# Two more transposes of a decoder trunk moved from TensorE to DMA, and one product of the norm weights moved ahead

## The chip, the core and the metric

The kernel runs on one core of a Trainium2 chip. A core has five engines that each work through their own list of instructions in order and wait for each other through semaphores: TensorE (PE, matrix products and transposes into PSUM), VectorE (DVE), ScalarE (ACT), GpSimd (POOL) and SyncE (SP, which here only issues DMA transfers). The metric is the time of one execution in microseconds (us); less is better.

## The reference

One layer: a norm, one wide projection, two branches (multi-scale pooling, sliding-window attention with a sink), one output projection, a second norm and a residual. 1024 tokens, width 1024, 8 heads of 64, two key/value heads. Cut to what is computed:

```python
h = rmsnorm(x, norm_pre)
pool_u, pool_gate, q, k, v, attn_gate = split(h @ w_in)
pool_out = pool_mixer(pool_u, pool_w, pool_scale) * silu(pool_gate)
# 128-query blocks, keys of this block and of the one before, ALiBi bias, a sink logit per head
probs = softmax(concat([scores + bias, sink]))[..., :-1]
attn_out = (probs @ v) * silu(attn_gate)
y = concat([pool_out, attn_out]) @ w_out
x = x + rmsnorm(y, norm_post)
```

## The kernel before, in words

Everything between x and y is kept transposed, channels on the 128 partitions and tokens along the free axis. To keep float32 accuracy at float16 speed, each operand of a large product is split into a high and a low float16 part (a scaled copy on ACT, then the difference on DVE), and each product is three passes (high*high, high*low, low*high).

**Tokens.** x comes in eight tiles of 128 tokens. `norm_scan` (ACT, with a small DVE and a small POOL step behind it) and `norm_scale` (DVE, line 241) normalize a tile to `h`. `flip` (line 250) transposes it on PE in float32, eight 128x128 blocks into two PSUM banks. `land_hi` (ACT, line 254) and `land_lo` (DVE, line 261) take it from there into `hT`, the float16 pair that all projections read.

**Weights.** A slice of `w_in` (128 columns) is loaded, its absolute sum taken on ACT (`bound_w`, line 91), spread over the partitions by a PE transpose (`spread`, line 82), and turned on DVE into a power of two (`scale_w`, lines 87 to 77, 213). Then ACT writes the high part (`high_w`, line 219) and DVE the low part (`low_w`, line 223).

**Units.** The projection is cut into 34 units `proj(ch, half)`: 24 matmuls of 128x512 at line 290 into one of the two PSUM banks of `ps_acc`. Unit s+2 therefore can't start before unit s has been taken out of its bank (`land_slot`; for a q slice by ACT and then DVE, lines 94 and 95). Units 0 to 4 are k and the four q slices for tokens 0 to 511, units 5 to 9 the same for tokens 512 to 1023, then pool gates, pool inputs (u) and attention gates. `v_tile` (line 272) makes v for one token tile.

**Attention.** From unit 5 on, two units carry one block n of 128 queries: `score_mm` (PE), `score_land` (DVE, lines 369 to 380), `exps` (ACT, line 387), `turn` and `turn_low` (ACT line 397, DVE line 402), which make a float16 pair of the probabilities. One DMA transpose on SP (line 406) turns it into `full`. POOL cuts out the two masked parts (`mask`, lines 425 and 429). PE multiplies by v (`pv_mm`, line 453) into the one bank of `ps_pv`. The reciprocals of the softmax sums are spread by POOL to 128x512 (line 411), turned on PE in float32 through the same `ps_pv` bank (`divide`, line 440), and copied by ACT with v's scale into `cat` (line 441). `pv_land` (DVE, line 463) multiplies both.

**Order.** The order on each engine is the order in which the code is written (`manual_schedule`); no scheduler changes it. `middle()` runs between the two halves of a unit's matmuls: weight scales, `divide` and the pooling products (`mixed`, line 506) stand there. Of the pooling branch, DVE makes window sums (lines 489 to 501), and the product of a slice needs the last of them.

## Time and profile before

| | before |
|---|---|
| time, median of 3 runs | 345.78 us (345.5 to 347.47) |
| the profiled execution, its own time | 346.77 us |
| its span, first to last instruction | 345.1 us |
| PE busy | 323.6 us, 94% of the span |
| DVE, ACT, POOL busy | 199.1, 168.9, 66.2 us |
| mean granted TensorE clock | 0.989 of full speed |

A share of 94% says that PE seldom stands still, not that it alone sets the end: an engine that is 50% busy can be the late one in a stretch where it and a third engine wait for each other in turn. So the profile is read by stretches, with the question which wait ends last. All times in the rows below are counted from the start of the span.

### The profile page before, as it was taken

What the parts mean: (1) busy time and instruction counts of PE and PEld (TensorE: products, weight loads), DVE (VectorE), ACT (ScalarE), POOL (GpSimd) and SP (SyncE); (2) the same over time, 40 slices, a digit from 0 to 9 for tenths busy, and PEclk for the clock granted to TensorE, in tenths of its full rate; (3) what the DMA queues carried; (4) which work ended last, traced back from release to release, by engine and by line L of the source; (5) the groups of instructions that cost most, each with busy time, mean ns of one, the idle gap of its engine ahead of it and who ended that gap; (6) DMA issues with size and microseconds to landing.
All of it is one profiled execution on the core that took longest, in us unless ns stands there. A gap on an engine that the chain in (4) does not pass through costs nothing.

```text
span 345.1 us, 5054 instructions
## 1 busy us (share of the span) xinstructions
PE 323.6 (94%) x1913; PEld 166.4 (48%) x1913; DVE 199.1 (58%) x423; ACT 168.9 (49%) x368; POOL 66.2 (19%) x73
## 2 busy tenths in 40 slices
PE   4689999999999999999979998799999999999993
PEld 2588556545444445445434443344444444444442
DVE  4976771537697445796979567793563633410222
ACT  4966831275656685878484443354463433211011
POOL 1100303000132344050423000000000333212330
PEclk9969999999999999999999999999999999999999
DMA  7986240001437367395240892010000241233111
GB/s 280 255 230 159 86 123 0 2 19 44 122 122 208 120 164 179 66 181 126 62 122 0 291 245 76 0 63 0 0 2 0 68 150 59 90 123 122 61 63 61
DMA packets 52090, 35.73 MB, mean 104 GB/s; under 512 B 35041, under 2 KB 45793, under 8 KB 52066
## 3 DMA queue, kind: packets, MB, share of 16 engines
q1 hardware_dynamic: 52064, 35.40, 37.1%
q8 instruction: 15, 0.25, 0.3%
q14 instruction: 9, 0.07, 0.1%
q10 hardware_dynamic: 2, 0.00, 0.0%
HBM read 27.01 MB, written 4.19 MB: 90 GB/s over the span
## 4 chain that ended last, share of the span: by engine, by line
PE 46%; DVE 19%; issue 16%; ACT 9%; POOL 6%; DMA 2%; POOLq 0%; DVEq 0%; SPq 0%; ACTq 0%
PE acc L290 30%; POOL o L639 5%; ACT st L387 4%; PE pv L272 3%; PE y L272 3%; DVE whl L223 3%; DVE st L375 2%; PE tp L250 2%; DVE win L489 2%; PE acc L272 2%; PE sc L358 2%; DVE sc L374 2%; DVE o L636 2%; PE pvo L453 1%; DVE negm L380 1%
## 5 line engine op out<-in xcount | busy, mean ns | idle before, releaser
L290 PE MATMUL acc<-hT,whl 128*128 128x512 f16 x792 | 176.7, 379 | 1.1 <-ACT gt L529 1.1
L290 PEld LDWEIGHTS <-whl 128*128 128x128 f16 x792 | 76.6, 98 | 93.9 <-issue 8.3
L272 PE MATMUL y<-wo,chl 128*128 128x512 f16 (+2 forms) x408 | 83.6, 366 | 0.0
L272 PEld LDWEIGHTS <-chl 128*128 128x128 f16 x408 | 39.0, 98 | 43.5
L219 ACT ACTIVATE whl<-wraw,ws 128x1024 f16<-128x1024 f32 x18 | 20.4, 1148 | 34.6 <-DVE wu L213 22.4
L609 ACT ACTIVATE junk<-y 128x512 bf16<-128x512 f32 (+2 forms) x17 | 9.7, 572 | 54.9 <-PE y L272 54.9
L387 ACT ACTIVATE st<-st,negm 128x129 f32<-128x129 f32 x64 | 24.8, 390 | 12.6 <-DVE negm L380 9.6
L611 DVE SCALAR_TENSOR_TENSOR eps_of<-yss,eps_of 128x1 f32<-128x1 f32 x17 | 3.2, 185 | 45.9 <-ACT junk L609 45.9
L631 POOL TENSOR_TENSOR yf<-eps_of,mhalf 128x1 f32<-128x1 f32 x7 | 3.9, 551 | 119.2 <-DVE eps_of L611 119.2
L223 DVE SCALAR_TENSOR_TENSOR whl<-wraw,ws,whl 128x1024 f16<-128x1024 f32 x18 | 23.7, 1327 | 0.0
L402 DVE SCALAR_TENSOR_TENSOR ph<-st,ph 128x1024 f16<-128x1024 f32 x8 | 9.8, 1226 | 21.6 <-ACT ph L397 21.6
L91 ACT ACTIVATE whl<-wraw 128x1024 bf16<-128x1024 f32 x18 | 18.8, 1049 | 1.5 <-DMA wraw<-in_w_in_dram 1.5
L639 POOL TENSOR_TENSOR o<-o,xr 128x512 f32<-128x512 f32 x14 | 17.5, 1269 | 9.1 <-DVE o L636 9.1
L425 POOL TENSOR_SCALAR_AFFINE_SELECT own<-full 128x2048 f16<-128x2048 f16 x7 | 14.5, 2071 | 22.9 <-DMA full<-ph 22.9
L411 POOL COPY r<-sums 128x512 f32<-128x512 f32 x8 | 4.9, 612 | 67.7 <-DVE sums L409 45.8
L250 PE MATMUL tp<-ident,h 128*128 128x128 f32 x64 | 10.9, 331 | 6.6 <-DVE h L241 3.4
L95 DVE SCALAR_TENSOR_TENSOR chl<-cat,cs,chl 128x1024 f16<-128x1024 f32 x8 | 10.3, 1284 | 10.2 <-ACT chl L94 10.2
L94 ACT ACTIVATE chl<-cat,cs 128x1024 f16<-128x1024 f32 x8 | 9.2, 1148 | 13.7 <-DVE cs L77 13.7
L375 DVE SCALAR_TENSOR_TENSOR st<-sc,qu,bias 128x256 f32<-128x256 f32 x32 | 15.2, 484 | 1.0
L429 POOL TENSOR_SCALAR_AFFINE_SELECT full<-full 128x2048 f16<-128x2048 f16 x7 | 14.4, 2055 | 0.5
L250 PEld LDWEIGHTS tp<-ident,h 128*128 128x128 f32 x64 | 9.1, 172 | 7.9 <-DVE h L241 3.8
L358 PE MATMUL sc<-kT,qT 64*128 64x256 f16 (+1 forms) x192 | 11.6, 263 | 0.6 <-DVE qT L95 0.4
(109 smaller groups left out, 371.9 us busy)
## 6 DMA issues: line engine op xcount, KB each, us to landing
wraw<-in_w_in_dram SPq DMA_DIRECT2D x10, 512.0 KB, 5.1
x<-in_x_dram SPq DMA_DIRECT2D x8, 512.0 KB, 5.4
wraw<-in_w_in_dram SPq DMA_DIRECT2D x16, 256.0 KB, 4.6
woraw<-in_w_out_dram SPq DMA_DIRECT2D x8, 512.0 KB, 5.5
woraw<-in_w_out_dram SPq DMA_DIRECT2D x16, 256.0 KB, 6.8
xr<-in_x_dram SPq DMA_DIRECT2D x8, 512.0 KB, 3.7
out_dram<-o SPq DMA_DIRECT2D x16, 256.0 KB, 2.0
post<-in_norm_post_dram SPq DMA_DIRECT2D x1, 512.0 KB, 4.2
```

The lines of the kernel that those rows point to most:

```text
L91: nc.scalar.activation(junk, src, AF.Abs, accum_out=m)
L219: nc.scalar.activation(whl[ch][:, 0], raws[ch], AF.Copy, scale=halves[ch])
L223: nc.vector.scalar_tensor_tensor(w[:, 1], raws.pop(ch), s, w[:, 0], op0=ALU.mult, op1=ALU.subtract)
L250: nc.tensor.transpose(flips[tt][b][:, block_of(i)], h[:, block_of(4 * b + i)], ident)
L272: nc.tensor.matmul(acc, a, b, start=i == 0, stop=i == len(pairs) - 1)
L290: nc.tensor.matmul(acc, w[:, a, k, :], hT[:, b, k, half_of(half)], start=k == 0 and i == 0, stop=k == KT - 1 and i == 2,)
L358: nc.tensor.matmul(banks[kv][:, ci, k0:, :], qT[rows, a, 2 * pr + ci, block_of(n)], kT[rows, b, (n - 1 + k0) * P : (n + 1) * P], start=i = ...
L375: nc.vector.scalar_tensor_tensor(st[:, hs, :P], sc[:, :, 0 if n else 1, :], qu[:, 2 * pr : 2 * pr + 1], (bias if n else bias0)[:, hs, :], ...
L387: nc.scalar.activation(st[:, h, :], st[:, h, :], AF.Exp, bias=negm[:, h : h + 1], accum_out=sums[:, h : h + 1],)
L425: nc.gpsimd.affine_select(o, f, pattern=[[0, 16], [1, P]], compare_op=ALU.is_ge, fill=0.0, base=0, channel_multiplier=-1,)
L429: nc.gpsimd.affine_select(f, f, pattern=[[0, 16], [-1, P]], compare_op=ALU.is_ge, fill=0.0, base=-1, channel_multiplier=1,)
L639: nc.gpsimd.tensor_tensor(o[:, hs], o[:, hs], xr[:, hs], op=ALU.add)
```

## The change

Three edits.

1. `gains()`: the product that spreads the norm weights' maximum stands between the products of the two halves of the weights, and on DVE the copy of the second half stands behind the three small scale operations.
2. Token tiles 4 to 7 are no longer turned on PE. `swing` makes the float16 pair first (ACT cast, DVE difference, both in SBUF) and turns it by one DMA transpose straight into `hT`. The steps around it are written in another order, and the three small loads of constants stand behind the last of these transposes on SP.
3. The reciprocals are scaled by 4096, split into a float16 pair on POOL, spread (two copies), turned by a DMA transpose, and added up by POOL into `cat`. PE's transposes and ACT's copy go away; v's scale is applied in `pv_land`.

```diff
-        for half in range(2):
-            nc.tensor.matmul(rows[half], ones, pre[:, half_of(half)], start=True, stop=True)
+        nc.tensor.matmul(rows[0], ones, pre[:, half_of(0)], start=True, stop=True)
         nc.tensor.matmul(most, ones, m, start=True, stop=True)
+        nc.tensor.matmul(rows[1], ones, pre[:, half_of(1)], start=True, stop=True)
         nc.vector.tensor_copy(grow[:, half_of(0)], rows[0])
-        nc.vector.tensor_copy(grow[:, half_of(1)], rows[1])
 ...
+        nc.vector.tensor_copy(grow[:, half_of(1)], rows[1])
 ...
+    def swing(tt):
+        h = h_tiles.pop(tt)
+        hh = work("hh").bitcast(F16).rearrange("p (a d) -> p a d", a=2)
+        nc.scalar.copy(hh[:, 0], h)
+        nc.vector.tensor_tensor(hh[:, 1], h, hh[:, 0], op=ALU.subtract)
+        nc.sync.dma_start_transpose(
+            hT[:, :, :, block_of(tt)].rearrange("p a k t -> p (a k) t"),
+            hh.rearrange("p a d -> p (a d)"),
+        )
 ...
         nc.vector.reciprocal(sums, sums)
-        r = t2.tile([P, 512], F32, tag="t2", name="r")
-        nc.gpsimd.tensor_copy(
-            r.rearrange("p (c kv d) -> p c kv d", c=4, kv=2),
-            sums.rearrange("p (kv c) -> p c kv", kv=2).unsqueeze(3).broadcast_to([P, 4, 2, HD]),
+        nc.gpsimd.tensor_scalar(r8, sums, 4096.0, 0.0, op0=ALU.mult, op1=ALU.add)
+        nc.gpsimd.tensor_copy(rp[:, 0], r8)
+        nc.gpsimd.tensor_tensor(rp[:, 1], r8, rp[:, 0], op=ALU.subtract)
+        r = t2.tile([P, 2, 512], F16, tag="t2", name="r")
+        for a in range(2):
+            nc.gpsimd.tensor_copy(
+                r[:, a].rearrange("p (c kv d) -> p c kv d", c=4, kv=2),
+                rp[:, a].rearrange("p (kv c) -> p c kv", kv=2).unsqueeze(3)
+                .broadcast_to([P, 4, 2, HD]),
+            )
+        rt = t2.tile([P, 2, 512], F16, tag="t2", name="rt")
+        nc.sync.dma_start_transpose(
+            rt.rearrange("p a (c t) -> p (a c) t", t=P), r.rearrange("p a j -> p (a j)")
         )
 ...
     def divide(n):
-        r = att_r.pop(n)
-        rb = ps_pv.tile([P, 512], F32, tag="pv", name="rb")
-        for c in range(4):
-            nc.tensor.transpose(rb[:, block_of(c)], r[:, block_of(c)], ident)
-        nc.scalar.activation(
-            cat[:, 4:8, block_of(n)], rb.rearrange("p (c t) -> p c t", t=P), AF.Copy, scale=vo
-        )
+        rt = att_r.pop(n).rearrange("p a (c t) -> p a c t", t=P)
+        nc.gpsimd.tensor_tensor(cat[:, 4:8, block_of(n)], rt[:, 0], rt[:, 1], op=ALU.add)
 ...
-        nc.vector.tensor_tensor(dst, pv.rearrange("p (c t) -> p c t", t=P), dst, op=ALU.mult)
+        nc.vector.scalar_tensor_tensor(
+            dst, pv.rearrange("p (c t) -> p c t", t=P), vo, dst, op0=ALU.mult, op1=ALU.mult
+        )
 ...
         low_w(QS[1])
-        load_constants()
         v_tile(0)
 ...
         bound_w(QS[2])
+        swing(4)
         norm_scale(5)
         unit(1)
         bound_w(QS[3])
         norm_scan(6)
         spread_w((QS[2], QS[3]))
-        flip(4)
-        flip(5)
-        norm_scan(7)
+        swing(5)
         norm_scale(6)
-        land_hi(4)
-        land_hi(5)
         scale_w((QS[2], QS[3]))
-        land_lo(4)
         high_w(QS[2])
         high_w(QS[3])
+        norm_scan(7)
+        low_w(QS[2])
         unit(2)
-        land_lo(5)
+        low_w(QS[3])
+        land_unit(1)
+        swing(6)
         norm_scale(7)
-        land_unit(1)
-        low_w(QS[2])
-        low_w(QS[3])
-        flip(6)
-        flip(7)
-        land_hi(6)
-        land_lo(6)
+        swing(7)
+        load_constants()
         unit(3)
-        land_hi(7)
-        land_lo(7)
         land_unit(2)
         v_tile(4)
```

On VectorE, around the scale of the weight slices q2 and q3 (`amall` to `wu`; `h_616` is tile 6, `h_662` tile 7, `qT` the taking out of unit 1, `whl` x2 the low parts of q2 and q3). Before:

```order
L241 SCALAR_TENSOR_TENSOR h_616<-x_254,rstd,grow 128x1024
L87 TENSOR_REDUCE amall<-spread 128x1
L73 TENSOR_SCALAR wp<-amall 128x1
L76 TENSOR_SCALAR wp<-wp 128x1
L77 RECIPROCAL ws<-wp 128x1
L213 TENSOR_TENSOR wu<-wp,gsc 128x1
L261 TENSOR_TENSOR hT<-tp,hT 128x4x128 x4
L241 SCALAR_TENSOR_TENSOR h_662<-x_321,rstd,grow 128x1024
L95 SCALAR_TENSOR_TENSOR qT<-acc,qT 128x512
L223 SCALAR_TENSOR_TENSOR whl<-wraw,ws,whl 128x1024 x2
```

Now (`h_550` is tile 5, `h_594` tile 6):

```order
L271 TENSOR_TENSOR hh<-h_550,hh 128x1024
L241 SCALAR_TENSOR_TENSOR h_594<-x_254,rstd,grow 128x1024
L87 TENSOR_REDUCE amall<-spread 128x1
L73 TENSOR_SCALAR wp<-amall 128x1
L76 TENSOR_SCALAR wp<-wp 128x1
L77 RECIPROCAL ws<-wp 128x1
L213 TENSOR_TENSOR wu<-wp,gsc 128x1
L235 TENSOR_SCALAR ms<-ss,gsq 128x1
L223 SCALAR_TENSOR_TENSOR whl<-wraw,ws,whl 128x1024 x2
L95 SCALAR_TENSOR_TENSOR qT<-acc,qT 128x512
L271 TENSOR_TENSOR hh<-h_594,hh 128x1024
```

The low part of tile 5 now stands ahead of the scale (so does that of tile 4, further up), and the taking out of unit 1 stands behind both low weight parts instead of ahead of them.

On ScalarE in the same place (`whl,as` are the absolute sums of q2 and q3, `junk,ss` the norm scans of tiles 6 and 7). Before:

```order
L91 ACTIVATE whl,as<-wraw 128x1024 x2
L233 ACTIVATE junk,ss<-x_254 128x1024
L233 ACTIVATE junk,ss<-x_321 128x1024
L254 CAST hT<-tp 128x4x128 x4
L219 ACTIVATE whl<-wraw,ws 128x1024 x2
L94 ACTIVATE qT<-acc 128x512
```

Now:

```order
L91 ACTIVATE whl,as<-wraw 128x1024
L270 CAST hh<-h_424 128x1024
L91 ACTIVATE whl,as<-wraw 128x1024
L233 ACTIVATE junk,ss<-x_254 128x1024
L270 CAST hh<-h_550 128x1024
L219 ACTIVATE whl<-wraw,ws 128x1024 x2
L233 ACTIVATE junk,ss<-x_321 128x1024
L94 ACTIVATE qT<-acc 128x512
L270 CAST hh<-h_594 128x1024
```

Two casts stand ahead of the high weight parts, and the scan of tile 7 between these and the taking out of unit 1.

On GpSimd, the last two attention blocks. Before:

```order
L411 COPY r<-sums 128x512
L425 AFFINE_SELECT own<-full 128x2048
L429 AFFINE_SELECT full<-full 128x2048
L411 COPY r<-sums 128x512
L425 AFFINE_SELECT own<-full 128x2048
L429 AFFINE_SELECT full<-full 128x2048
```

Now, for the last block alone:

```order
L424 TENSOR_SCALAR r_2110<-sums 128x8
L425 CAST rp<-r_2110 128x8
L426 TENSOR_TENSOR rp<-r_2110,rp 128x8
L429 COPY r<-rp 128x512 x2
L448 AFFINE_SELECT own<-full 128x2048
L452 AFFINE_SELECT full<-full 128x2048
L461 TENSOR_TENSOR cat<-rt 128x4x128
```

One copy became five instructions, and a sum stands behind the two masks.

## Rows read from the trace of the kernel before

**Rows 1.** The page's first part: busy us, share, instructions of each engine.

```profile
PE 323.6 (94%) x1913; PEld 166.4 (48%) x1913; DVE 199.1 (58%) x423; ACT 168.9 (49%) x368; POOL 66.2 (19%) x73
```

**Rows 2.** Waits of PE: who waited for whom, us, times, longest us.

```profile
PE rb L440 <- DVE cat L463: 2.6, 2, 1.8
...
PE acc L290 <- ACT gt L529: 1.1, 1, 1.1
```

**Rows 3.** Timeline of DVE at the start: start us, us, instruction, idle before it.

```profile
6.09 0.69 DVE L179 COPY grow<-gain 128x512 f32<-128x512 f32 x1 [1.01 <-PE gain L176]
```

**Rows 4.** Timeline of PE around units 2 and 3.

```profile
39.74 5.34 PE L290 MATMUL acc<-hT,whl 128*128 128x512 f16 x24
44.92 1.91 PE L250 MATMUL tp<-ident,h 128*128 128x128 f32 x16
46.67 5.34 PE L290 MATMUL acc<-hT,whl 128*128 128x512 f16 x24
```

**Rows 5.** Timeline of ACT in the same stretch.

```profile
33.39 1.07 ACT L91 ACTIVATE whl<-wraw 128x1024 bf16<-128x1024 f32 x1
...
40.55 2.22 ACT L219 ACTIVATE whl<-wraw,ws 128x1024 f16<-128x1024 f32 x2
```

**Rows 6.** Timeline of DVE in the same stretch.

```profile
39.01 0.28 DVE L87 TENSOR_REDUCE amall<-spread 128x1 f32<-128x128 f32 x1
...
39.71 0.17 DVE L77 RECIPROCAL ws<-wp 128x1 f32<-128x1 f32 x1
...
43.43 0.68 DVE L95 SCALAR_TENSOR_TENSOR qT<-acc,qT 128x512 f16<-128x512 f32 x1
44.03 2.47 DVE L223 SCALAR_TENSOR_TENSOR whl<-wraw,ws,whl 128x1024 f16<-128x1024 f32 x2
```

**Rows 7.** Groups of instructions by form: xcount, busy us, mean ns of one, idle before.

```profile
L639 POOL TENSOR_TENSOR o<-o,xr 128x512 f32<-128x512 f32 x14 | 17.5, 1269 | 9.1 <-DVE o L636 9.1
...
L402 DVE SCALAR_TENSOR_TENSOR ph<-st,ph 128x1024 f16<-128x1024 f32 x8 | 9.8, 1226 | 21.6 <-ACT ph L397 21.6
...
L411 POOL COPY r<-sums 128x512 f32<-128x512 f32 x8 | 4.9, 612 | 67.7 <-DVE sums L409 45.8 <-ACT qT L94 16.5 <-DVE ug L478 5.4
```

**Rows 8.** The page's DMA issues: instruction, count, median us from issue to landing.

```profile
full<-ph SPq DMA_TRANSPOSE x8, 3.7
```

**Rows 9.** Busy time of the engines by stretch; PEclk, DMA share, GB/s at the end.

```profile
20.00:22.00 2.00, 2.00 (x20) 1.94 (x19) 2.00 (x4) 1.73 (x4) 0.00 (x0) 0.50 1.17 249
22.00:24.00 2.00, 2.00 (x24) 2.00 (x22) 1.36 (x2) 2.00 (x5) 0.00 (x0) 0.56 0.49 186
...
176.00:178.00 2.00, 0.22 (x2) 0.00 (x0) 1.46 (x4) 2.00 (x4) 0.28 (x1) 1.00 0.75 172
...
340.00:345.00 5.00, 0.00 (x0) 0.00 (x0) 1.61 (x3) 0.00 (x0) 0.55 (x1) 0.96 0.28 105
```

**Rows 10.** The chain that ended last, in order of time: start us, us, what.

```profile
121.29 0.44 PE rb L440 x4
```

**Rows 11.** Timeline of PE at the third pooling slice.

```profile
184.56 1.11 PE L506 MATMUL mixed<-res,pw 128*128 128x512 f32 x2
```

**Rows 12.** Timeline of DVE through attention blocks 5 to 7.

```profile
135.17 0.29 DVE L87 TENSOR_REDUCE amall<-spread 128x1 f32<-128x128 f32 x1 [3.52 <-PE spread L82]
...
171.41 0.69 DVE L495 SCALAR_TENSOR_TENSOR res<-win,ug 128x512 f32<-128x512 f32 x1
...
180.03 2.37 DVE L495 SCALAR_TENSOR_TENSOR res<-win,ug 128x512 f32<-128x512 f32 x1
182.44 1.85 DVE L500 TENSOR_TENSOR win<-win,invc 128x7 f32<-128x7 f32 x1
184.32 0.17 DVE L501 TENSOR_TENSOR res<-win,ug 128x7 f32<-128x7 f32 x1
```

**Rows 13.** Timeline of POOL at the masks of block 7.

```profile
179.40 2.46 POOL L425 TENSOR_SCALAR_AFFINE_SELECT own<-full 128x2048 f16<-128x2048 f16 x1 [3.12 <-DMA full<-ph]
181.93 2.34 POOL L429 TENSOR_SCALAR_AFFINE_SELECT full<-full 128x2048 f16<-128x2048 f16 x1
```

More of the change, by code (lines that the diff above doesn't have):

```diff
@@ L409, in turn_low @@
         nc.vector.reciprocal(sums, sums)
-        r = t2.tile([P, 512], F32, tag="t2", name="r")
-        nc.gpsimd.tensor_copy(
-            r.rearrange("p (c kv d) -> p c kv d", c=4, kv=2),
-            sums.rearrange("p (kv c) -> p c kv", kv=2).unsqueeze(3).broadcast_to([P, 4, 2, HD]),
+        r8 = small.tile([P, 8], F32, tag="r8", name="r8")
+        rp = small.tile([P, 2, 8], F16, tag="rp", name="rp")
+        nc.gpsimd.tensor_scalar(r8, sums, 4096.0, 0.0, op0=ALU.mult, op1=ALU.add)
[11 more added lines that the diff above has]
+            rt.rearrange("p a (c t) -> p (a c) t", t=P), r.rearrange("p a j -> p (a j)")
         )
         att_f[n] = full
-        att_r[n] = r
+        att_r[n] = rt
     def mask(n):
@@ L540, in scale_v @@
     def scale_v():
-        nc.vector.tensor_scalar(vo, wu[V], 2.0**7, None, op0=ALU.mult)
+        nc.vector.tensor_scalar(vo, wu[V], 2.0**-5, None, op0=ALU.mult)
     wo_raw = {}
```

## The prediction, made before the changed kernel had run

> **What bounds the kernel now.** I read the page first. PE is busy for 323.6 of 345.1 us [rows 1], so the first thought is that work taken from PE is time won. The waits of PE are the check: behind the start it waits for almost nothing but DVE and ACT, 2.6 us for the bank that `divide` shares with `pv_land`, 1.1 us for an ACT step of the gates [rows 2]. So PE is the bound, but by a narrow margin, and the question for every us that PE gives up is who is late next. For that I followed the engines' timelines in two places.
>
> The first is the start of the projection, 33 to 49 us. There ACT and DVE work through one chain: absolute sums, norm, landing of the transposes, weight scale, high part, low part [rows 5, 6]. Unit 3 starts on PE at 46.67, right behind 16 transposes that began at 44.92 [rows 4]. Its bank was free and its weights ready just before (the low parts ran from 44.03 to 46.5, [rows 6]).
>
> The second is attention blocks 5 to 7, 135 to 190 us. DVE waits for PE at 135.17, 3.52 us long [rows 12]; from there on DVE and ACT hand work to each other (scores, exponentials, low part, pooling sums), and where PE meets them again it waits: the longest of its 2.6 us, 1.8 us, is at the transposes of block 7 [rows 2]. At the third pooling product PE and DVE are level: the last write of its input ends at 184.49 [rows 12], PE starts at 184.56 [rows 11].
>
> **The change, part by part.**
>
> *Norm weights.* The scale operations no longer wait for the copy of the second half, 0.69 us at 6.09 [rows 3], but the copy still stands ahead of the first norm on DVE, and its product now comes later on PE. Between 0 and -0.7 us; I take -0.2, since only the three small operations change sides.
>
> *Tiles 4 to 7: what PE gives up.* Two stretches of 16 transposes go, each 1.75 us by the distance of starts [rows 4], 3.5 us in all. What replaces them on ACT and DVE costs the same there: a cast of a whole tile about one pass over 128x1024, 1.07 us [rows 5], the difference about 1.23 us, as the low half with the same operands [rows 7].
>
> *Tiles 4 to 7: where they now stand.* Both casts and both differences of tiles 4 and 5 are now ahead of the weight scale for q2 and q3, and the taking out of unit 1 is behind the low parts. I add up the chain from the last step that doesn't move, the absolute sum of q2 on ACT at 33.39 [rows 5]: that sum 1.07, cast of tile 4 1.07, its difference 1.23, norm of tile 5 1.23 (the same form [rows 7]), cast of tile 5 1.07, its difference 1.23, norm of tile 6 1.23, the scale from 39.01 to 39.88 0.87 [rows 6], two high parts 2.22 [rows 5], the scan of tile 7 1.07, two low parts 2.47, the taking out of unit 1 0.68 [rows 6]. That is 15.44 us, which ends at 48.8. Only then is the bank free that unit 3 writes. Unit 3 starts at 48.8 instead of 46.67: **+2.2 us** instead of a gain of 3.5. Each of the twelve steps may start some hundredths earlier or later than the end of the one before; I keep 1.7 to 2.7. What hid this work before was PE's own transposes, and they are gone.
>
> *The clock at that place.* Unit 2 needs the weights' sums, done near 38.2 in the same chain, so it runs from about 38.5 to 43.7 (5.34 us long, 5.2 to the next start [rows 4]). PE then stands still for 5.1 us. In the trace the granted clock stayed at 1.00 through an idle of 1.8 us (176 to 178 us) and had fallen within five idle us at the end (340 to 345 us, mean 0.96), and after the start's idle times it stood at 0.50, 1.2 GHz, while PE was fully busy from 20 us, and came back in the slice 22 to 24 us, whose mean of 0.56 puts the rise at 23.8 [rows 9]. I take it that the clock falls and that 3.8 us run at half speed: **+1.9 us**, with 0 as the other end.
>
> *The DMA transposes.* Four of the size of the one in the trace, which lands 3.7 us after its issue [rows 8]. The last, tile 7, is issued near 53.6 (48.8 plus three steps of 1.23 and a cast of 1.07), lands at 57.3, and is needed after unit 3, two v tiles and unit 4, near 64: hidden, with 6 us to spare. The constants and four weight loads are queued behind it on SP and land by 63; the sums that read the first of them are due some 4 us later. Nothing. Of the skill I weigh one figure here: the Trainium skill, VectorE: DVE Perf Modes, section on the three transpose paths, gives 1309 ns for one 128x128 block by DMA, 16 of which would be an estimated 20.9 us for a tile. The trace's 3.7 us for 16 blocks decides against that use of it.
>
> *Reciprocals, blocks 0 to 3.* PE gives up 0.44 us for each block [rows 10] and the shorter of its two waits, 2.6 - 1.8 = 0.8 us [rows 2]: 4 x 0.44 + 0.8, **-2.6 us**. This passes, since DVE has 3.52 us of idle time at 135.17 [rows 12] that may shrink; the lower end is -1.8, if the next mask is late where the bank was. ACT's copy and its idle time go too, off the path.
>
> *Reciprocals, blocks 4 to 7.* PE gives up 4 x 0.44 + 1.8 = 3.6 us more, but from 135 on the end of the pooling input on DVE decides, and DVE gains nothing: ACT's copy wasn't in its way. It gets more to wait for. At 180.03 a pooling sum that takes 0.69 us elsewhere took 2.37, and ended 0.54 us behind the first mask on POOL, and the next step, 7 elements wide, took 1.85 us and ended with the second mask [rows 12, 13]. DVE and POOL take turns there, an instruction at a time. POOL now has a sum behind the second mask, 1.27 us by the nearest row (same shape, float32 [rows 7]), and it comes before the last DVE write of the pooling input: +1.3. Ahead of the masks two copies of 0.61 stand where one stood [rows 7]; a two-operand step of DVE that meets one waits half of it on average, +0.3. Together **+1.6 us** at the third pooling product, between 0 (each falls into DVE's idle time) and 2.5 (1.27 and two whole copies).
>
> PE is 3.6 us ahead by then and ready at 181.0; it must wait to 186.2. That is again 5.2 us of standing still, so again the clock: **+1.9 us**, other end 0. What follows (the products of block 7, the release of the attention buffers, the loads of the output weights, the remaining units) starts from this product.
>
> **Sum.** -0.2 + 2.2 + 1.9 - 2.6 + 1.6 + 1.9 = +4.8 us. The profiled execution, a span of 345.1 and a time of 346.77 us, would become a span of 349.9 and 351.6 us; it lies 1.0 us above the median of the runs, 345.78, so the median becomes **350.6 us**, 1.4% slower. Less than 1% (3.5 us) either way I count as no change that can be told.
>
> **Rivals.**
>
> *PE sets the end everywhere.* Then all that it gives up counts: 3.5 + 8 x 0.44 + 2.6 + 0.2 = 9.8 us, 336.0 us. For it speaks the share of 94%; against it the chain above, which has no slack that could hide 5 us. 10%.
>
> *Only the first place holds.* If DVE isn't late in blocks 4 to 7, because POOL's sum lands in its waiting times and the masks come earlier, then -0.2 + 2.2 + 1.9 - 2.6 - 3.6 = -2.3, 343.5 us: not slower. What speaks against it is the level meeting at 184.5. 15%.
>
> *The places hold, the price is smaller.* The clock stays up at one or both, or the last write slips in ahead of POOL's sum: +1.0 without either loss of clock, +2.9 with one, 346.8 to 348.7 us. An idle of 5 us lies between the 1.8 us that left the clock alone and a five-us slice that it fell in, so this is near the forecast in weight. 30%.
>
> *DVE and POOL collide in every block.* If each new copy and sum of blocks 5 to 7 holds up a two-operand step of DVE for its whole length, it is 3 x (1.27 + 2 x 0.61) = 7.5 instead of 1.6 us, 356.5 us. It decides from the point where POOL's instruction starts first. Against it: DVE reads scores from PSUM while most of them run, and the one copy of before met no long step. 6%. The Trainium skill, SBUF — State Buffer, section on who interferes with whom, has the rule for this: a VectorE instruction with two SBUF inputs and a GpSimd instruction that reads SBUF exclude each other for a whole instruction, and the order of issue decides. The two stretched steps agree [rows 12, 13].
>
> *The transposes are slow.* At 20.9 us tile 7 would land at 74.5, 10.6 us behind its need: 361 us. Against it stands 3.7 us [rows 8]. 2%.
>
> **How the numbers follow.** The forecast as summed has 37%; its own range is 348.5 to 352.5. The range 343.0 to 353.0 takes in the second and third rival and leaves out the first, the last two and some of the edges, below 2 in 10. Faster by over 1% (below 342.3): the first rival and a little of the second, 0.12. Slower by over 1% (above 349.2): most of the forecast, a part of the third rival, the last two, 0.43. The rest, 0.45.
>
> **What would show it.** Unit 3 starts more than 2 us later than the 46.67 of before, PE idle for about 5 us ahead of it, waiting for DVE's taking out of unit 1; a granted clock of 0.5 behind it. The transposes land long before tile 4's v product. Blocks 0 to 3 come 0.44 us closer together. At the third pooling product PE waits again for DVE, whose last small step is stretched by POOL's new sum. I am wrong at the root if PE has no wait of several us in either place; in size if the clock stays at 1.00.

## The result: 10.7 us slower

| | before, on the same chip | after |
|---|---|---|
| time, median of 4 runs each | 346.09 us (345.5 to 347.47) | 356.78 us (354.99 to 359.25) |
| ratio | 1 | 1.031, 95% interval 1.024 to 1.038 |
| the profiled execution, its own time | 346.77 us | 359.25 us |
| its span | 345.1 us | 357.5 us |

The forecast was 350.6 us, and its range ended at 353.0. The profiled execution is the longest of the four; its span grew by 12.4 us.

The page of the changed kernel, engines, answers to [rows 1]: PE gave up 64 instructions, yet its busy time is 0.6 us longer, since some of what is left runs at half clock.

```profile
PE 324.2 (91%) x1849; PEld 161.4 (45%) x1849; DVE 203.3 (57%) x419; ACT 163.7 (46%) x356; POOL 88.2 (25%) x113
```

The waits of PE in the changed kernel (who waited for whom, us, times, longest) answer to [rows 2]. The wait for the bank (`rb`) is gone; five new ones stand in its place, in three stretches. ("issue" says that the profile shows nothing that PE waited for.)

```profile
PE mixed L526 <- DVE res L521: 5.6, 1, 5.6
PE acc L301 <- DVE qT L95: 5.2, 1, 5.2
...
PE pvo L471 <- POOL own L448: 1.7, 1, 1.7
PE mixed L526 <- issue: 1.6, 1, 1.6
...
PE pvo L471 <- POOL full L452: 1.2, 1, 1.2
```

Where the 12.4 us went is best read with fixed points on PE: unit 1, unit 5, the scores of block 5 (sc5), the third and the fourth pooling product, the end. Each is the start time of a row in PE's timeline; the runs of the next section are in the same table, by their names.

| us between | unit 1 starts | to unit 5 | to sc5 | to 3rd product | to 4th product | to the end |
|---|---|---|---|---|---|---|
| before | 32.71 | 31.59 | 66.54 | 53.72 | 7.76 | 152.8 |
| **after** | 31.85 | 36.19 | 68.27 | 57.73 | 10.55 | 152.9 |
| e1_tiles | 32.73 | 36.69 | 66.57 | 56.93 | 7.67 | 153.2 |
| e2_recip | 33.29 | 31.59 | 64.61 | 57.96 | 9.87 | 152.8 |
| e3_order | 31.23 | 28.52 | 65.86 | 57.72 | 10.16 | 152.9 |
| e4_no_turn | 31.95 | 36.27 | 65.98 | 56.19 | 10.79 | 153.2 |
| e5_sinks | 32.45 | 36.46 | 66.66 | 54.60 | 7.75 | 152.9 |
| e6_quarters | 32.58 | 36.63 | 65.84 | 51.54 | 7.74 | 154.3 |
| e7_order_pe | 31.74 | 28.52 | 66.67 | 57.02 | 7.67 | 152.9 |
| e8_all | 31.91 | 28.52 | 66.14 | 53.72 | 7.67 | 152.8 |
| e9_more | 32.54 | 31.68 | 66.59 | 57.14 | 7.67 | 152.7 |
| e10_all_dma | 33.70 | 28.54 | 65.89 | 51.65 | 7.75 | 154.2 |
| e11_gains | 32.79 | 31.59 | 66.55 | 53.71 | 7.76 | 152.7 |
| e12_fill | 32.65 | 33.78 | 64.57 | 57.92 | 10.58 | 152.9 |
| e13_more | 32.46 | 36.60 | 64.70 | 56.18 | 9.86 | 152.9 |
| e14_all_more | 32.05 | 29.03 | 64.45 | 51.41 | 7.75 | 154.5 |

The row of after against that of before: -0.9, +4.6, +1.7, +4.0, +2.8, +0.1. Unit 1 starts between 31.2 and 33.7 in these runs, in no order that a change explains, so the -0.9 is put down to the run.

**The first place** is as forecast. PE's timeline (start us, us, instruction, idle before it) answers to [rows 4]:

```profile
47.99 7.76 PE L301 MATMUL acc<-hT,whl 128*128 128x512 f16 x24 [5.17 <-DVE qT L95]
55.59 2.84 PE L283 MATMUL pv<-whl,hT 128*128 128x128 f16 x48
```

and DVE's timeline to [rows 6]: scale, low parts and the taking out of unit 1 now follow the tiles' steps.

```profile
40.53 0.28 DVE L87 TENSOR_REDUCE amall<-spread 128x1 f32<-128x128 f32 x1
...
44.87 2.47 DVE L223 SCALAR_TENSOR_TENSOR whl<-wraw,ws,whl 128x1024 f16<-128x1024 f32 x2
47.25 0.69 DVE L95 SCALAR_TENSOR_TENSOR qT<-acc,qT 128x512 f16<-128x512 f32 x1
```

**The second place**, blocks 0 to 3, was not forecast. PE waits twice for the masks of block 2, then the scores of block 4 take 2.74 us where they take 1.48 elsewhere:

```profile
118.59 0.84 PE L471 MATMUL pvo<-own,vst 128*64 128x512 f16 x6 [1.75 <-POOL own L448]
120.66 1.01 PE L471 MATMUL pvo<-full,vst 128*64 128x512 f16 x6 [1.24 <-POOL full L452]
121.61 2.74 PE L369 MATMUL sc<-kT,qT 64*128 64x256 f16 x24
```

**The third place**, the third pooling product, answers to [rows 11, 12, 13]. PE, then DVE, then POOL:

```profile
174.45 1.10 PE L526 MATMUL mixed<-res,pw 128*128 128x512 f32 x2 [1.64 <-issue]
...
194.04 2.05 PE L526 MATMUL mixed<-res,pw 128*128 128x512 f32 x2 [5.64 <-DVE res L521]
195.88 4.65 PE L301 MATMUL acc<-hT,whl 128*128 128x512 f16 x12
```

```profile
141.42 1.69 DVE L213 TENSOR_TENSOR wu<-wp,gsc 128x1 f32<-128x1 f32 x1
...
171.60 1.91 DVE L380 COPY st<-sinks 128x8 f32<-128x8 f32 x1
...
173.87 0.49 DVE L386 SCALAR_TENSOR_TENSOR st<-sc,qu,bias 128x256 f32<-128x256 f32 x1
...
186.97 3.29 DVE L509 TENSOR_TENSOR win<-win 128x525 f32<-128x525 f32 x2
190.29 2.37 DVE L515 SCALAR_TENSOR_TENSOR res<-win,ug 128x512 f32<-128x512 f32 x1
192.70 0.99 DVE L520 TENSOR_TENSOR win<-win,invc 128x7 f32<-128x7 f32 x1
```

```profile
170.78 2.70 POOL L448 TENSOR_SCALAR_AFFINE_SELECT own<-full 128x2048 f16<-128x2048 f16 x1 [1.29 <-DMA full<-ph]
...
187.70 2.01 POOL L448 TENSOR_SCALAR_AFFINE_SELECT own<-full 128x2048 f16<-128x2048 f16 x1 [1.82 <-DMA full<-ph]
189.78 2.35 POOL L452 TENSOR_SCALAR_AFFINE_SELECT full<-full 128x2048 f16<-128x2048 f16 x1
192.10 1.58 POOL L461 TENSOR_TENSOR cat<-rt 128x512 f32<-128x512 f16 x1
```

The same steps of DVE in the kernel before:

```profile
135.95 0.55 DVE L213 TENSOR_TENSOR wu<-wp,gsc 128x1 f32<-128x1 f32 x1
...
164.93 0.16 DVE L369 COPY st<-sinks 128x8 f32<-128x8 f32 x1
...
178.55 1.44 DVE L489 TENSOR_TENSOR win<-win 128x525 f32<-128x525 f32 x2
```

The copy of the sink logits into the tile of block 7's scores, 8 elements a partition and called the sinks' copy below, takes 1.91 us, 0.17 in the other blocks, and ends when the first mask of block 6 does. It also explains the wait of 1.64 us for which the profile names nothing: the first pooling product takes its PSUM bank from the four that the scores of block 7 hold, and it starts 0.1 us behind DVE's first step that has read one out (173.87 to 174.36), which the sinks' copy held up. The same distance of 0.1 us stands in e2_recip, e3_order and e12_fill, with waits of 1.7 to 1.9 us. At the third product it costs nothing that can be seen, for there PE stands 5.64 us for DVE in any case.

The clock, by stretches (busy time of PE, PEld, DVE, ACT, POOL; granted clock, DMA share, GB/s): behind each of the three stalls it is near 0.5, which is 1.2 GHz.

```profile
48.00:52.00 4.00, 4.00 (x10) 1.42 (x10) 2.89 (x3) 1.54 (x2) 0.00 (x1) 0.50 0.47 90
...
121.00:124.00 3.00, 3.00 (x30) 1.68 (x25) 2.44 (x6) 3.00 (x6) 1.50 (x5) 0.53 0.12 46
...
194.00:197.00 3.00, 2.96 (x5) 1.10 (x6) 2.71 (x5) 0.00 (x0) 0.00 (x0) 0.50 0.00 0
```

### The profile page after: what moved, and what is told of

Read it like the earlier page. It is cut to its first block, busy times and chain, and to the rows that moved or that the text cites. A ratio compares the mean times of both kernels' runs of the same rounds, so it can differ in the third digit from the quotient of the medians.

```text
span 357.5 us, 4970 instructions
## 1 busy us (share of the span) xinstructions
PE 324.2 (91%) x1849; PEld 161.4 (45%) x1849; DVE 203.3 (57%) x419; ACT 163.7 (46%) x356; POOL 88.2 (25%) x113
## 4 chain that ended last, share of the span: by engine, by line
PE 42%; DVE 20%; issue 17%; ACT 11%; POOL 7%; DMA 2%; POOLq 0%; DVEq 0%; ACTq 0%
PE acc L301 28%; POOL o L659 5%; DVE win L509 3%; PE y L283 3%; ACT st L398 3%; PE sc L369 2%; DVE whl L223 2%; PE acc L283 2%; ACT whl L219 2%; PE pvo L471 2%; DVE st L386 2%; DVE h L241 2%; DMA full<-ph 2%; PE pv L283 2%; DVE o L656 1%
## 5 line engine op out<-in xcount | busy, mean ns | idle before, releaser
L301 PE MATMUL acc<-hT,whl 128*128 128x512 f16 x792 | 180.6, 386 | 6.3 <-DVE qT L95 5.2
L301 PEld LDWEIGHTS <-whl 128*128 128x128 f16 x792 | 77.7, 99 | 104.9 <-issue 20.6
L223 DVE SCALAR_TENSOR_TENSOR whl<-wraw,ws,whl 128x1024 f16<-128x1024 f32 x18 | 22.8, 1279 | 0.0
L526 PE MATMUL mixed<-res,pw 128*128 128x512 f32 x16 | 9.4, 671 | 8.1 <-DVE res L521 5.6
L424 POOL TENSOR_SCALAR r<-sums 128x8 f32<-128x8 f32 x8 | 1.6, 199 | 56.2 <-DVE sums L420 34.7
L237 POOL TENSOR_TENSOR rstd<-ms,mhalf 128x1 f32<-128x1 f32 x8 | 5.3, 664 | 39.9 <-DVE ms L235 36.2
L369 PE MATMUL sc<-kT,qT 64*128 64x256 f16 (+1 forms) x192 | 12.9, 282 | 0.6 <-DVE qT L95 0.4
```

The source lines that it names most:

```text
L223: nc.vector.scalar_tensor_tensor(w[:, 1], raws.pop(ch), s, w[:, 0], op0=ALU.mult, op1=ALU.subtract)
L301: nc.tensor.matmul(acc, w[:, a, k, :], hT[:, b, k, half_of(half)], start=k == 0 and i == 0, stop=k == KT - 1 and i == 2,)
L369: nc.tensor.matmul(banks[kv][:, ci, k0:, :], qT[rows, a, 2 * pr + ci, block_of(n)], kT[rows, b, (n - 1 + k0) * P : (n + 1) * P], start=i = ...
```

## The experiments

Times are medians of 4 to 12 runs, each against the kernel before on the same chip (346.25 to 346.53 us). The stretches in the table are those of one profiled run each.

### The parts alone: e1_tiles, e2_recip, e11_gains

e1_tiles, the changed kernel with the old reciprocals:

```diff
-        nc.gpsimd.tensor_scalar(r8, sums, 4096.0, 0.0, op0=ALU.mult, op1=ALU.add)
...
+            nc.tensor.transpose(rb[:, block_of(c)], r[:, block_of(c)], ident)
```

> The reciprocals are turned on PE as before; the norm weights and the tiles are as changed. Theory (the two parts cost separately): unit 3 starts near 48, unit 5 near 68.0 as in the changed kernel, and from there on everything is as before: 346 + 3.7 = about 350. Rival (the loss behind unit 5 comes from the other alignment of the engines that the tiles bring, not from the reciprocals): about 356.

Measured 355.31 us, ratio 1.025 (1.024 to 1.027): the rival's number. Unit 1 to unit 5 takes 5.1 us longer than before, as in the changed kernel (4.6), blocks 0 to 4 are as before (66.57), and 3.2 us more are lost ahead of the third product. DVE and POOL of this run show at what:

```profile
170.08 1.91 DVE L380 COPY st<-sinks 128x8 f32<-128x8 f32 x1
```

```profile
169.55 2.41 POOL L436 TENSOR_SCALAR_AFFINE_SELECT own<-full 128x2048 f16<-128x2048 f16 x1 [3.10 <-DMA full<-ph]
```

It is the same copy as in the changed kernel, with the reciprocals on PE.

e2_recip, the kernel before with the new `turn_low`, `divide`, `pv_land` and `scale_v`:

```diff
-            nc.tensor.transpose(rb[:, block_of(c)], r[:, block_of(c)], ident)
...
+        nc.gpsimd.tensor_tensor(cat[:, 4:8, block_of(n)], rt[:, 0], rt[:, 1], op=ALU.add)
```

> Only the reciprocals are changed; norm weights and tiles as before. Theory (the two parts cost separately): unit 5 at 64.3 as before, then 1.7 us lost in blocks 0 to 3 and 6.8 us in blocks 4 to 7: about 354. Rival (alignment): within 2 us of before, 344 to 348.

Measured 350.68 us, ratio 1.012 (1.009 to 1.014), between the two. In blocks 0 to 4 the reciprocals gain 1.9 us (64.61 against 66.54), so the loss there in the changed kernel isn't theirs alone; the later stretches lose 4.2 and 2.1. The two parts, +9.0 and +4.4 us, make more than the whole. In the profiles the surplus lies ahead of the third product: 3.2 and 4.2 us there alone, 4.0 together, and the sinks' copy takes 1.91 and 1.90 us in the two, which the changed kernel pays once.

e11_gains, the kernel before with the norm weights' edit:

```diff
+        nc.tensor.matmul(most, ones, m, start=True, stop=True)
+        nc.tensor.matmul(rows[1], ones, pre[:, half_of(1)], start=True, stop=True)
```

> The kernel before with the norm weights' edit alone. Theory (three small steps change sides, and the transposes of tile 0 come a little earlier): -0.2 us, 346.2. Rival (the whole copy of 0.69 us leaves the path, unit 1 starts at 31.9 instead of 32.7): 345.5 to 345.7.

345.84 us against 346.29, ratio 0.999 (0.997 to 1.000), and unit 1 at 32.79: between the two expectations, a gain of a few tenths at most.

### The first place: e3_order, e7_order_pe, e12_fill

e3_order, the changed kernel with this order:

```diff
         spread_w((QS[2], QS[3]))
-        swing(5)
-        norm_scale(6)
         scale_w((QS[2], QS[3]))
+        land_unit(1)
         high_w(QS[2])
         high_w(QS[3])
+        low_w(QS[2])
+        norm_scale(6)
+        swing(5)
         norm_scan(7)
-        low_w(QS[2])
         unit(2)
         low_w(QS[3])
-        land_unit(1)
```

> The changed kernel with eight steps written in another order: scale and first low part of q2 and q3, and the taking out of unit 1, ahead of the cast and difference of tile 5. Theory (the chain ahead of unit 3 is what PE waits for): unit 3 starts at 42.9 instead of 48.0 and runs 5.3 instead of 7.8 us, unit 5 at about 60.5 instead of 68.0, and the end 7 us earlier: about 350. Rival (blocks 4 to 7 are set by DVE and POOL and take the gain back): 354 or more.

348.86 us, ratio 1.007 (1.005 to 1.009). PE runs units 2 and 3 without a break, and unit 5 comes 28.52 us behind unit 1 instead of 36.19, so the chain was the cause. The end comes 7.9 us earlier, so blocks 4 to 7 took nothing of it back; they lose what they lose in the changed kernel (57.72 and 10.16).

e7_order_pe, the same with the old reciprocals:

```diff
+        land_unit(1)
...
+            nc.tensor.transpose(rb[:, block_of(c)], r[:, block_of(c)], ident)
```

> The tiles turned by DMA in the order of the third run (scale, low part and taking out ahead of tile 5), the reciprocals on PE as before. Theory: unit 5 at about 60.5 against 64.3 before, then as in the run with the tiles alone, 3.4 us lost again between blocks 6 and 7 if the mask of block 6 meets the copy of the sinks, none if not: 342.5 to 346. Rival (what is won at the start is taken back by DVE in full): 346 to 348.

346.45 us, ratio 1.000 (0.999 to 1.002): just above the theory's range and inside the rival's. Unit 1 to unit 5 takes 28.52 instead of 31.59 us, 3.1 less, and the stretch ahead of the third product 57.02 instead of 53.72, 3.3 more: the sinks' copy takes 1.91 us here too. The tiles by DMA, well ordered, gain about what that copy then costs.

e12_fill, the changed kernel with PE kept busy in the stall:

```diff
         load_constants()
+        fill = bank("fill")
+        products(fill, [(whl[QS[1]][:, 0, k % KT, :], hT[:, 0, k % KT, half_of(0)]) for k in range(20)])
         unit(3)
```

> The changed kernel with 20 matmuls of 128x512 ahead of unit 3 that nobody reads, in the 5.2 us in which PE stands still (work added, none left out). Theory (the clock falls because PE stands still): unit 3 still starts near 48.0, but runs at full clock, 5.3 instead of 7.8 us, and the time is 2.4 us less, about 354.3. Rival (unit 3 is slow for another reason, its operands or its bank): 356 to 357.

353.86 us (350.45 to 355.06). PE's timeline: the filler ends 0.85 us before unit 3, and unit 3 runs at full clock.

```profile
43.47 4.48 PE L283 MATMUL fill<-hT,whl 128*128 128x512 f16 x20
48.80 5.34 PE L301 MATMUL acc<-hT,whl 128*128 128x512 f16 x24 [0.85 <-DVE qT L95]
```

Unit 1 to unit 5 takes 33.78 instead of 36.19 us: the clock cost 2.4 us, the late work 2.2. This run's blocks 0 to 4 take 64.57 us, a second effect that was not meant; e13_more below explains it.

### The second and third place: who is late on POOL and DVE

e4_no_turn, the changed kernel without the transposes of the reciprocals (`divide` sums the pair as spread):

```diff
-        nc.sync.dma_start_transpose(
-            rt.rearrange("p a (c t) -> p (a c) t", t=P), r.rearrange("p a j -> p (a j)")
-        )
...
-        att_r[n] = rt
+        att_r[n] = r
```

> The changed kernel without the DMA transposes of the reciprocals: POOL's sum reads the pair as it was spread (left out: the turning of the reciprocals, 8 transfers). Theory (these transfers hold up the one of the probabilities and the masks behind it): the mask of block 2 starts 3.8 instead of 6.0 us after the issue of its transfer, that of block 4 3.8 instead of 5.1, PE's waits of 1.7 and 1.2 us for the masks are gone, and the time is 3 to 4 us less, about 353. Rival (the transfer of the probabilities is late on its own, as in block 6 of before with 4.6 us of waiting): less than 1 us.

356.33 us (354.87 to 358.15): the rival. The mask of block 2 still starts 5.52 us behind the issue, at 115.99 for 110.47, that of block 4 5.43. The second transfer isn't what delays the first. In this profile, though, unit 5 to sc5 takes 65.98 us, 2.3 less than in the changed kernel, with masks nearly as late: PE's first wait is 1.03 instead of 1.75 us, and the clock doesn't fall behind it. The medians, 356.33 and 356.78, don't show it.

e5_sinks, e1_tiles with one more edit:

```diff
-        nc.vector.tensor_copy(st[:, :, P], sinks)
+        nc.scalar.copy(st[:, :, P], sinks)
```

> The run with the tiles alone, and with the copy of the sinks into the scores' tile made by ACT instead of DVE. Theory (DVE's copy is locked out while POOL's mask of block 6 runs, 1.91 us instead of 0.17; before, this mask came 1.5 us later, since the transfer it waits for was held up by a fetch of instructions): the step from the reduce of block 6 to that of block 7 goes back from 16.7 to 15.0 us, PE's wait of 3.6 us for the bank and the low clock behind it shrink, and the time goes from 355.3 to about 352, the 5.1 us of unit 5 being left. Rival (the copy is only the first DVE step behind the mask, and the next takes over the wait): 354.5 to 355.5.

353.00 us, ratio 1.019 (1.017 to 1.021): between the two and nearer the theory, 2.3 us less than e1_tiles. From the reduce of block 6 to that of block 7 it takes 14.96 us again, and PE waits 1.8 us at the transposes of block 7 as in before. The next step on DVE, which reads PSUM, isn't held up though the mask runs (from 170.04 to 172.42):

```profile
170.54 0.42 DVE L385 COPY_PREDICATED sc<-own_key,sc 128x256 f32<-128x256 uint16 x1
170.99 0.48 DVE L386 SCALAR_TENSOR_TENSOR st<-sc,qu,bias 128x256 f32<-128x256 f32 x1
```

e6_quarters, the changed kernel with each mask in four instructions:

```diff
-        nc.gpsimd.affine_select(
-            o, f, pattern=[[0, 16], [1, P]], compare_op=ALU.is_ge, fill=0.0,
-            base=0, channel_multiplier=-1,
-        )
+        for j in range(0, 16, 4):
+            nc.gpsimd.affine_select(
+                o[:, j : j + 4], f[:, j : j + 4], pattern=[[0, 4], [1, P]],
+                compare_op=ALU.is_ge, fill=0.0, base=0, channel_multiplier=-1,
+            )
...
```

> The changed kernel with each of POOL's masks cut into four instructions of a quarter. Theory (a DVE step waits for the POOL instruction that runs, so its wait has the length of one instruction): of the 9.2 us by which seven DVE steps are stretched, less than 3 are left, PE's wait of 5.6 us at the third pooling product is cut to 2 or 3, and the time is 348 to 352 instead of 356.8. Rival (DVE pays for the whole time of the masks, however they are cut, since each of its steps meets a new one): 355 to 358.

350.20 us, ratio 1.011 (1.009 to 1.013), 6.6 us less than the changed kernel. DVE and PE at the third product:

```profile
184.34 1.00 DVE L517 SCALAR_TENSOR_TENSOR res<-win,ug 128x512 f32<-128x512 f32 x1
185.38 0.48 DVE L522 TENSOR_TENSOR win<-win,invc 128x7 f32<-128x7 f32 x1
185.89 0.55 DVE L523 TENSOR_TENSOR res<-win,ug 128x7 f32<-128x7 f32 x1
```

```profile
186.59 1.10 PE L528 MATMUL mixed<-res,pw 128*128 128x512 f32 x2 [1.43 <-DVE res L523]
187.52 2.75 PE L301 MATMUL acc<-hT,whl 128*128 128x512 f16 x12
```

Each step waits 0.3 to 0.4 us instead of 1.7, PE waits 1.43 instead of 5.64, and the clock stays up there. A DVE step waits for one POOL instruction, and the length of that instruction is the price.

e9_more, the kernel *before*, with 33 matmuls of units 1 and 2 cut in two:

```diff
+                for j in range(2 if 0 < k < cut else 1):
+                    n = 256 if 0 < k < cut else 512
+                    nc.tensor.matmul(
+                        acc[:, j * n : (j + 1) * n], w[:, a, k, :],
...
-            accs[s] = proj(ch, half)
+            accs[s] = proj(ch, half, cut={1: 7, 2: 6}.get(s, 0))
```

> The kernel before with 33 of the 48 matmuls of units 1 and 2 cut into two halves each: the same products, 33 matmuls and 33 weight loads more on PE, far ahead of the attention blocks. Theory (before is lucky: the fetch of PE's instructions falls into the transfer of block 6 and delays its mask until DVE has copied the sinks; 66 instructions move the fetch 7 us ahead, out of the transfer): the mask of block 6 starts 3.8 instead of 5.3 us after the issue of its transfer, the sinks' copy takes 1.9 instead of 0.16 us, PE waits 3.5 instead of 1.8 us at the transposes of block 7, and the time is 349 to 350.5, though nothing is changed there. Rival (the late mask has another cause and doesn't matter): 346.3 to 347.0, the cut matmuls' own cost.

350.10 us, ratio 1.010 (1.008 to 1.013): 3.8 us slower, by something that costs under 0.1 us where it stands (31.68 against 31.59). All is level with before up to block 6. There the trace shows why. DMA from 160 to 166 us in 40 slices, GB/s; first the kernel before, then e9_more:

```profile
GB/s 10 0 0 0 0 0 0 0 0 0 0 0 150 290 294 283 294 294 287 292 280 287 292 372 141 7 0 0 0 7 9 10 10 9 0 0 0 0 0 0
...
q8 instruction: 1, 0.02, 1.0%
```

```profile
GB/s 126 0 0 0 0 0 0 0 0 0 0 10 193 282 285 297 285 292 292 285 295 290 285 292 103 10 0 0 0 0 0 0 0 0 0 0 0 0 0 0
...
q8 instruction: 1, 0.02, 1.2%
```

Both move the probabilities of block 6 at some 290 GB/s from 161.8 to 163.8. In before one packet of a queue of the kind "instruction" (q8, 0.02 MB) starts at 163.5, 2.9 us behind the issue, and a rest of the transfer then comes at 10 GB/s from 164.3 to 165.1; only behind it does the mask start. In e9_more that packet starts at 160.1, ahead of the issue at 160.6, and there is no such rest. POOL, in the same order:

```profile
165.88 2.01 POOL L425 TENSOR_SCALAR_AFFINE_SELECT own<-full 128x2048 f16<-128x2048 f16 x1 [4.59 <-DMA full<-ph]
```

```profile
164.43 2.34 POOL L428 TENSOR_SCALAR_AFFINE_SELECT own<-full 128x2048 f16<-128x2048 f16 x1 [3.17 <-DMA full<-ph]
```

The sinks' copy stood at 164.93 in before, ahead of the mask, and took 0.16 us; in e9_more it stands at 164.89, behind it:

```profile
164.89 1.91 DVE L372 COPY st<-sinks 128x8 f32<-128x8 f32 x1
```

PE then waits 3.56 instead of 1.83 us at the transposes of block 7, and the clock falls. The fetch moved by 3.4 us, not by the 7 expected, which was enough.

### Put together: e8_all, e10_all_dma, e13_more, e14_all_more

e8_all has the edits of e7_order_pe, e5_sinks and e6_quarters. 

```diff
+        land_unit(1)
...
+        nc.scalar.copy(st[:, :, P], sinks)
...
+        for j in range(0, 16, 4):
```

> All three together: tiles by DMA in the mended order, reciprocals on PE, sinks copied by ACT, masks in quarters. Theory: unit 5 at 60.5, no lock longer than a quarter of a mask, so nothing of that is given back: 341 to 343, faster than both kernels. Rival (PE then waits for the bank of the weighted values as before, and the quarters cost POOL time): 344 to 346.

342.73 us, ratio 0.989 (0.987 to 0.991). e10_all_dma is e8_all with the reciprocals by DMA:

```diff
-            nc.tensor.transpose(rb[:, block_of(c)], r[:, block_of(c)], ident)
...
+        nc.gpsimd.tensor_tensor(cat[:, 4:8, block_of(n)], rt[:, 0], rt[:, 1], op=ALU.add)
```

> The eighth run with the reciprocals turned by DMA, as in the changed kernel: tiles in the mended order, sinks on ACT, masks in quarters. Theory (PE's end in blocks 4 to 7 is set by DVE, which gains nothing from the reciprocals, and pays for POOL's copies and sum): 342.5 to 344.5, no better than the 342.7 with the reciprocals on PE. Rival (only the locks ate the gain of 8 x 0.44 + 2.6 = 6.1 us): 337 to 340.

342.52 us, ratio 0.989 (0.986 to 0.991): the theory's number, at the lower end, for the wrong reason. The third product comes 2.1 us sooner behind sc5 (51.65 against 53.72), but the rest is spent elsewhere: unit 1 started 1.8 us later in this profile (343.45 us, the longest of the five runs), blocks 0 to 4 take 65.89 us, and the last stretch 1.4 us more, since PE waits 2.80 instead of 1.49 us, until 208.8, for a reduce of the weight scales on DVE and the clock falls behind it (so it does in e6_quarters and e14_all_more). A fetch falls into the transfers of blocks 2 and 4 (5.78 and 5.59 us to the mask).

e13_more and e14_all_more are the changed kernel and e10_all_dma with the cut matmuls of e9_more:

```diff
-            accs[s] = proj(ch, half)
+            accs[s] = proj(ch, half, cut={1: 7, 2: 6}.get(s, 0))
```

> The changed kernel with the cut matmuls of the ninth run: 66 instructions more on PE in units 1 and 2, which move the fetches some 7 us ahead of where they are, out of the transfers of blocks 2 and 4. Theory (the fetch holds up the mask of block 2, PE waits for it and falls to half clock): the masks of blocks 2 and 4 start 3.8 to 4.1 instead of 6.0 and 5.1 us after their issue, PE goes from the scores of block 0 to those of block 5 in 66.4 us, as with the reciprocals alone, instead of 70.1, and the time is 353 to 354.5. Rival (tiles and reciprocals together hold up the mask): 70 us for that stretch, 356 to 357.5.

355.06 us (352.85 to 357.88), ratio 1.026 (1.022 to 1.030), between the two by its median. The trace decides: in the changed kernel the transfer of block 2 is broken off (DMA from 110 to 116 us, GB/s),

```profile
GB/s 10 0 0 0 0 0 0 0 0 0 0 137 283 294 280 278 275 241 31 109 0 0 0 0 0 2 9 9 10 9 15 275 288 295 283 294 270 285 292 294
...
q8 instruction: 1, 0.02, 1.0%
```

and in e13_more, from 111 to 117 us, with the fetch at 107, it isn't:

```profile
GB/s 0 0 0 0 0 0 0 0 0 0 51 256 292 292 288 288 290 292 290 290 290 287 243 46 0 0 0 0 0 0 14 171 222 220 208 201 203 207 208 229
```

The masks of blocks 2 and 4 start 4.16 and 4.15 us behind their issue instead of 6.04 and 5.10, PE waits 1.06 us there instead of 2.99, the clock stays up, and unit 5 to sc5 takes 64.70 instead of 68.27 us, as with the reciprocals alone. The times themselves, 354.99 to 359.25 us in the changed kernel and 352.85 to 357.88 here, don't tell the two apart.

> The tenth run with the same cut matmuls. Theory (the fetch in the transfer of block 2 took back what the reciprocals gave): blocks 0 to 4 take 66.4 instead of 67.7 us, and the time is 340 to 341.5. Rival (DVE sets the pace from block 4 on and takes it back): 342 to 343, as with the reciprocals on PE.

341.05 us (340.23 to 341.29), ratio 0.984 (0.983 to 0.986): faster than both kernels and the fastest version here. Unit 5 to sc5 takes 64.45 us (the expectation's 66.4 and 67.7 count from the scores of block 0, 1.8 us ahead of unit 5).

## Why the prediction was wrong

*Norm weights, -0.2.* Right within what can be told.

*Unit 3 late, +2.2.* Right, by its own chain: unit 1 to unit 3 took 16.14 us instead of 13.96, +2.18. e3_order and e12_fill show the cause.

*The clock there, +1.9.* Right in kind, it measured 2.4 (e12_fill: unit 3 takes 5.34 instead of 7.76 us), which at half speed is 4.8 us of low clock instead of the 3.8 taken over from the start.

*The DMA transposes of the tiles.* Right: the v product of tile 4 started behind unit 3 without a wait, and the rival of slow transposes is out.

*Reciprocals, blocks 0 to 3, -2.6.* **This is the step that failed first.** It said "This passes" and looked for the danger at DVE; for a late mask its lower end, -1.8, allowed no more than the 0.8 us of the old wait for the bank. By itself it would have passed, with 1.9 of the 2.6 us (e2_recip; 0.97 us went into a first wait for the mask of block 2). In the changed kernel it became +1.7, because PE, ahead of its old place, now waits for the mask of block 2, and that mask was 2 us late: the tiles' transposes were gone from PE, and a fetch of instructions fell into the transfer of that block (e13_more). The profiles with both parts part this in two. Without a fetch in that transfer unit 5 to sc5 takes 64.6 to 64.7 us (e12_fill, e13_more). With one and the clock up it takes 65.9 to 66.0 (e3_order, e4_no_turn), so the late masks cost 1.3. In the changed kernel's own profile the clock fell too, and it takes 68.27, 2.3 more. So -2.6 became about -0.6 in two profiles and +1.7 in the third. How often the clock falls there in runs without a profile isn't seen: the medians of the changed kernel and e13_more, 356.78 and 355.06, lie closer than the 3.6 us between their two profiles, and both kernels scatter over 4 to 5 us.

*Blocks 4 to 7, +1.6.* Right in the mechanism, the lock between DVE and POOL, and mis-sized: it measured +4.0. **This is the term that failed by its size.** I priced the two new POOL steps and took the masks as they stood in [rows 12, 13], so what the masks do more was put at nothing. From sc5 to the third product the DVE steps that meet a POOL instruction take 8.5 us longer in all than the same steps elsewhere in the run, 4.6 in the kernel before, and the 3.9 between the two make up the +4.0. The new sum accounts for 1.0 and the copies for 0.2 more than the one copy of before, together not far from the 1.6. The masks account for the other 2.7, 6.8 us instead of 4.2: they held up the sinks' copy of block 7 by 1.74 us, a weight scale of 128x1 behind block 4 by 1.55 (before by 0.41), and a window sum of block 7 by 1.85 that was free before. The sinks' copy is no price of the new steps: the kernel before had escaped the mask through a late transfer, and e9_more brings it on by moving the fetch. The prediction doesn't name this copy at all. e5_sinks and e6_quarters settle that the lock is the cause. Of the Trainium skill, SBUF — State Buffer, section on who interferes with whom, I used the half on two SBUF inputs. That section of the Trainium skill also says that a VectorE instruction in a two-port mode contends with GpSimd too, that a copy can enter such a mode, and that the one that comes second "fully blocks". The trace agrees as far as it goes: the copy has one input, in SBUF, and its 1.91 us end with the mask; the mode itself isn't in the trace.

*The clock there, +1.9.* Right in kind, 2.8 in this profile, 2.1 in e2_recip.

*The sum.* Measured less forecast, term by term in the profile: -0.7 at the start, 0.0, +0.5, +4.3, +2.4, +0.9, and 0.1 behind the fourth product, 7.5 us; that is 12.4 less 4.8, but for roundings. The top of the range, 353.0, had no room for the loss in blocks 0 to 3 or for what the masks do more. Of the rivals, "DVE and POOL collide in every block" had 356.5 us, near the result by luck, by the right lock and the wrong instructions: in the changed kernel the new copies stretched two DVE steps by 0.29 and 0.34 us and the sum two by 0.20 and 0.83, and e6_quarters, 6.6 us faster, kept all copies and sums. What the prediction held against this rival, that the one copy of before met no long step, was misread: from 147.44 to 148.05 that copy held up a low weight part, which takes 1.28 us elsewhere.

```profile
147.42 1.71 DVE L223 SCALAR_TENSOR_TENSOR whl<-wraw,ws,whl 128x1024 f16<-128x1024 f32 x1
```

**What stays open.** Why the end of a transfer waits for the fetch. In how many runs the clock falls behind the masks of block 2. That q8 fetches PE's instructions is inferred, from its moving with 66 instructions on PE (e9_more, e13_more). Why unit 1 starts at 31.2 to 33.7 us.

## What to carry to other kernels

A tuned kernel's time can rest on an accident: before taking a short row as the price of a step, look whether a neighbour that it could collide with came late in that one place, and count what it costs if it doesn't. Where work goes off the bound engine, list every wait that this engine had just missed, and the lengths of the other engines' instructions that it can now meet: cutting the long GpSimd masks in four was worth 6.6 us here. An idle time of PE of 3.5 to 5.6 us cost 1.5 to 2.8 us again in clock.

## What the hardware showed that was not expected

- Instructions are fetched by DMA while the kernel runs, and the transposes feel it. Of the 112 transfers of the probabilities in the 16 profiles (blocks 1 to 7), the mask starts 3.7 to 4.4 us behind the issue in 92. In 16 a packet of q8 starts 1.1 to 3.0 us behind the issue, and in all of these it is 5.1 to 6.0 us; in the other 4 (5.8 to 6.0) a packet of q8 comes at 3.5 to 3.8 us and one of a second instruction queue, q14, at 1.1 to 1.2. Alone, neither did that: 3.8 us with q8 at 3.5, 4.2 to 4.4 with q14 at 1.1 to 1.5.
- A DVE copy of 128x8 between two SBUF tiles takes 0.17 us, and 1.91 when it meets a whole GpSimd mask (0.53 and 0.62 with masks in quarters); on ACT it takes 0.19.
- PE's clock stayed up through idles of 1.8 us (e8_all, e5_sinks) and fell behind one of 2.8 (e6_quarters, e10_all_dma, e14_all_more) and of 3.5 (e7_order_pe, e9_more). In the changed kernel it also fell behind 1.75 and 1.24 us with 0.84 us of matmuls between them; behind 0.92 and 1.23 (e3_order) and 1.03 and 1.24 (e4_no_turn) in the same place it stayed up.
